# One accumulator, and a last stage on chip, at the end of a mixture-of-experts layer

## The chip, the cores and the metric

The kernel runs on one core of one Trainium2 chip. The number that counts is device time in microseconds (us), as the median of three runs. All times inside the kernel come from one profiled execution and are counted from its first instruction. Engines are named as the profile names them: PE is the matmul engine (PEld its weight loads), DVE the vector engine, ACT the scalar engine, POOL the GpSimd engine, SP the sync engine, which here only issues DMAs.

## The reference, cut to what matters

The block is a token mixer followed by a mixture of experts (MoE) on 512 tokens of 1024 values. Only the end of the MoE is touched by the change:

```python
def _moe(h, ...):                       # 64 experts, each token goes to 8 of them
    ...
    yb = lax.map(expert_block, (xb, block_e)).reshape(n_slots, d)
    routed = jax.ops.segment_sum(yb * slot_w[:, None].astype(yb.dtype), slot_tok, num_segments=t + 1)[:t]
    shared = (jax.nn.silu(xt @ w_sh_gate_l) * (xt @ w_sh_up_l)) @ w_sh_down_l
    return (routed + shared).reshape(b, l, d)
...
    x = x + g2 * _rmsnorm(_moe(h2, *moe_p), norm_ffn_post[i])
```

So every expert's rows are scaled and added to the rows of their tokens; then each token's sum is normalized by its root mean square, multiplied by a vector (`g2p` in the kernel) and added to the token's value from before the MoE (`x1`), which gives the output.

## The kernel before

The MoE works through 65 blocks: one of 128 rows for each of the 64 experts (`e` from 0 to 63), and one extra block (`e == NE`, 64) for the rows that overflow a block. Further overflow blocks, if there are any, run in a loop whose count the chip reads from memory (`For_i(0, cnt)`, L1459). In this data the count is zero: 65 blocks' matmuls stand in the profile.

The loop over `e` is unrolled, and step `e` holds pieces of several blocks: the gate and up projections of block `e` (`proj`), the transposes of block `e+2`'s gathered rows (`make`), the conversion of weights ahead (`convert`), the down projection of block `e-1` (`down`), and the gather of block `e+4`'s rows (`prepare`). Weights come through SP's queue, three blocks ahead; those of the extra block are gathered through POOL's queue. POOL also issues the gathers of rows, and, for each block, an indirect DMA that adds the block's 128 rows into a [512, 1024] accumulator in DRAM (L1272, `compute_op=OP.add`), called the scatter below.

Two accumulators are kept, `accd[0]` and `accd[1]`. The blocks alternate between them, and the last four all go to the second. `accd[0]` begins as the shared expert's output, `accd[1]` as zeros (a memset and four writes, L1152 to L1154). The order of instructions that touch one DRAM tensor is kept by semaphores: a scatter waits until the earlier scatter into the same accumulator has landed.

`accd[0]` is read back (`m0`, L1453) in step 62, together with two of the four tiles of `x1`. After the last scatter comes the loop for further blocks; with a count of zero, every engine jumps over the body and waits until everything issued so far is done. Behind it `accd[1]` is read (L1476), the two sums are added (L1478), squared and summed on ACT (L1481), scaled and raised to the power -1/2 (`rsqrt`: L126 on DVE, L127 on POOL), multiplied (L1484), and added to `x1`: by an adding DMA for two of the four token tiles (L1486), on DVE for the other two (L1488), which are then written (L1489). L1507 is the end of the program, where all engines meet.

`down` splits a block's 1024 columns in two halves in PSUM; DVE scales the first into `y` (L1271), ACT the second (L1269). `pa`, `pi` and `pc` hand out PSUM banks (3, 3 and 2). Instructions of an engine run in the order that the compiler's scheduler gave them, which need not be that of the text; `tc.issue_after(x)` puts an instruction behind `x` on its engine. Matmul operands in `F32R` run in one pass; those in `F32` take more.

Of the kernel before, what the change touches and what calls it, by code (L numbers as in the profile page):

```python
# [19 lines left out]
D = 1024  # L20
# [51 lines left out]
class K:  # L72
# [912 lines left out]
    def phaseO(self):  # L985
# [7 lines left out]
        self.accd = [dp.tile([512, 1024], F32, name=f"acc{i}") for i in range(2)]  # L993
# [79 lines left out]
        def shared_down(t):  # L1073
            y = self.rawp.tile([128, 1024], F32, name="y", tag="raw")
            for c in range(2):
                ps = self.pa()
                for k in range(2):
                    nc.tensor.matmul(ps, sgs[t][:, k * 128:k * 128 + 128], wsh[2][:, k, c * 512:c * 512 + 512], start=k == 0, stop=k == 1)  # L1078
                nc.scalar.copy(y[:, c * 512:c * 512 + 512], ps)
            nc.scalar.dma_start(self.accd[0][t * 128:t * 128 + 128], y)  # L1080
# [77 lines left out]
    def phaseM(self):  # L1158
# [26 lines left out]
        def load(e, n, wix=None):  # L1185
            if e > NE:
                return
            t = raw(e, n)
# [72 lines left out]
        def down(aT, sx, ws, wd, acc):  # L1261
            y = self.rawp.tile([128, 1024], F32, name="y", tag="raw")
            for c in range(2):
# [6 lines left out]
                else:  # L1270
                    ts(y[:, 0:512], ps, ws, None, op0=OP.mult)  # L1271
            nc.gpsimd.indirect_dma_start(self.accd[acc][:, :], bass.IndirectOffsetOnAxis(ap=sx, axis=0), y[:, :], None,  # L1272
                                         bounds_check=511, oob_is_err=False, compute_op=OP.add)

# [140 lines left out]
        def extra_list(wi, px, colx):  # L1415
            ps = self.pi()
            pv = ps[:, 0:6].rearrange("p (e j) -> p e j", e=1)
            onehot_mm(pv[:, 0], lambda c: px[:, c:c + 1], lambda c: colx[:, c, 0])
            sl = [q.tile([128, 1], dt, name=nm, bufs=2) for dt, nm in ((F32, "sl_t"), (I32, "sl_i"), (F32, "sl_w"))]
            slot_of(pv, 1, sl)  # L1420
            return wi, sl[1], sl[2]

        x = lambda e: [XT[e][:, h] for h in range(2)]
        for e in range(NE + 2):
            if e == 3:
                ranks()
# [15 lines left out]
            if e > 0:  # L1442
                down(aT, SL[e - 1], W[e - 1], raw(e - 1, 2), 1 if e - 1 > NE - 4 else (e - 1) % 2)
                load(e + 2, 2)
            make(e + 2, 1)
            prepare(e + 4)
            if e == NE - 2:

                halves = lambda w: [w[:, i * 1024:i * 1024 + 1024] for i in range(2)]
                m0 = halves(raw(e, 0)) + halves(raw(e, 1))  # L1450
                x1 = halves(raw(e + 1, 0)) + halves(raw(e + 1, 1))
                for t in range(4):
                    nc.sync.dma_start(m0[t], self.accd[0][t * 128:t * 128 + 128])  # L1453
                for t in range(2, 4):
                    nc.sync.dma_start(x1[t], self.out[t * 128:t * 128 + 128])


        cnt = nc.values_load(nx[0:1, 0:1], min_val=0, max_val=62)
        with tc.For_i(0, cnt) as _:  # L1459
            wi, ix, ws = extra_list(*extra_cols())  # L1460
            xT, xg = xtile(), gather(ix)
            for c in range(2):
                turn(xT, c, xg)
            for n in range(3):
                load(NE, n, wi)
            w = [conv(raw(NE, n), tt, 1024) for n in range(2)]
# [3 lines left out]
            down(turn_act(act(pgu[:, 0:256], pgu[:, 256:512])), ix, ws, raw(NE, 2), 1)  # L1470


        m = halves(raw(NE, 0)) + halves(raw(NE, 1))
        r = q.tile([128, 4], F32, name="fr")
        for t in range(4):
            (nc.scalar if t % 2 else nc.sync).dma_start(m[t], self.accd[1][t * 128:t * 128 + 128])  # L1476
        for t in range(4):
            tt(m[t], m[t], m0[t], op=OP.add)  # L1478
            self.d("moe", m[t], t)
            junk = q.tile([128, 1024], BF, name="xT", bufs=2)  # L1480
            nc.scalar.activation(junk, m[t], AF.Square, accum_out=r[:, t:t + 1])  # L1481
            self.rsqrt(r[:, t:t + 1], r[:, t:t + 1], 1.0 / D, EPS)
        for t in range(4):
            nc.vector.scalar_tensor_tensor(m[t], m[t], r[:, t:t + 1], g2p, op0=OP.mult, op1=OP.mult)  # L1484
            if t < 2:
                nc.gpsimd.dma_start(self.out[t * 128:t * 128 + 128], m[t], accum_op=OP.add)  # L1486
            else:
                tt(m[t], m[t], x1[t], op=OP.add)  # L1488
                (nc.scalar if t % 2 else nc.sync).dma_start(self.out[t * 128:t * 128 + 128], m[t])  # L1489
# [22 lines left out]
```

## Time and profile before

| | |
|---|---|
| median of 3 runs | 1406.16 us (1405.65 to 1406.91) |
| the profiled execution, whole | 1415.91 us |
| its span, first to last instruction | 1414.1 us |
| busy share of the span: PE, DVE, ACT, POOL | 94%, 64%, 46%, 29% |
| last matmul ends at | 1381.5 us |

The profiled execution is 0.7% longer than the median, and 1.8 us of it lie outside the span. Shares of the whole span hide that nothing runs on PE in the last 32 us.

### The profile page before, as it was taken

The page shows a single profiled execution, that of the slowest core. Times are in us where ns is not written, and L with a number is a line of the kernel's source. Part 1 is how long each engine was busy: PE and PEld are TensorE (multiplying, and loading weights), DVE is VectorE, ACT ScalarE, POOL GpSimd, SP SyncE. Part 2 cuts the span into 40 slices and gives each one's busy share as a digit, 9 for nine tenths or more (in the row PEclk, how much of TensorE's full clock was granted, in tenths as well). Part 3 has the DMA queues.
Part 4 walks back from the last instruction along what each step waited for, and adds up shares of the span by engine and source line. Part 5 has one row for each costly group of instructions (what it writes and reads, how often), then busy time and mean ns, then how long its engine had stood idle before and what let it go on. Part 6 is the DMA issues. An engine that isn't in the chain of part 4 may idle for free.

```text
span 1414.1 us, 20716 instructions
## 1 busy us (share of the span) xinstructions
PE 1324.8 (94%) x7848; PEld 1074.7 (76%) x7848; DVE 906.7 (64%) x1270; ACT 653.4 (46%) x926; POOL 409.6 (29%) x330
## 2 busy tenths in 40 slices
PE   6999988899999999999999999999999999999990
PEld 1678866798787777778888787878788888878770
DVE  5645796457676555547668666666666666666543
ACT  5533432553333222334355555555656565555531
POOL 0315544865321000003222222222222222224312
PEclk9899998999999999999999999999999999999995
DMA  7554411102316577575699999999999999999954
GB/s 275 181 141 117 121 56 35 52 16 74 88 49 179 178 214 223 152 259 195 249 386 349 352 370 345 373 351 364 362 366 361 368 364 361 367 364 338 326 183 127
DMA packets 137817, 340.51 MB, mean 241 GB/s; under 512 B 28218, under 2 KB 83038, under 8 KB 112756
## 3 DMA queue, kind: packets, MB, share of 16 engines
q1 hardware_dynamic: 110952, 289.46, 57.2%
q0 software_dynamic: 19584, 38.99, 10.9%
q10 hardware_dynamic: 7180, 10.72, 2.2%
q8 instruction: 63, 1.03, 0.3%
q14 instruction: 38, 0.31, 0.1%
HBM read 326.59 MB, written 48.31 MB: 265 GB/s over the span
## 4 chain that ended last, share of the span: by engine, by line
PE 43%; DMA 7%; issue 1%; ACT 1%; POOL 1%; DVE 0%; DVEq 0%; SPq 0%; ACTq 0%; POOLq 0%
PE cs L1267 13%; PE acc L111 7%; PE acc L113 7%; PE acc L112 7%; DMA w<-in_w_up_dram 4%; PE ci L1236 3%; DMA w<-in_w_gate_dram 2%; PE ci L1066 2%; PE acc L1078 1%; PE acc L1256 1%; DMA w<-acc 1%; POOL fr L127 0%; DMA acc<-y,slots 0%; DMA acc<-y,sl_i 0%; ACT wh L1171 0%
## 5 line engine op out<-in xcount | busy, mean ns | idle before, releaser
L111 PE MATMUL acc<-wh,xT 128*128 128x256 f32 x1040 | 302.2, 291 | 0.0
L113 PE MATMUL acc<-wh,xT 128*128 128x256 f32 x1040 | 291.0, 280 | 0.0
L112 PE MATMUL acc<-wl,xT 128*128 128x256 f32 x1040 | 290.6, 279 | 0.0
L1173 DVE TENSOR_TENSOR wl<-w,wh 128x2048 fp32r<-128x2048 f32 x88 | 201.5, 2291 | 76.2 <-PE acc L112 75.2
L1267 PE MATMUL cs<-wd,aT 128*128 128x512 f32 x520 | 234.6, 594 | 4.5 <-DMA wd<-in_w_down_dram 3.6
L1272 POOL DMA_INDIRECT acc<-y,slots x64 | 101.9, 1593 | 466.5 <-ACT y L1269 427.8
L1171 ACT CAST wh<-w 128x2048 fp32r<-128x2048 f32 x88 | 167.5, 1904 | 99.5 <-PE acc L113 70.2
L111 PEld LDWEIGHTS acc<-wh,xT 128*128 128x128 f32 x1040 | 196.6, 189 | 0.2 <-issue 0.2
L112 PEld LDWEIGHTS acc<-wl,xT 128*128 128x128 f32 x1040 | 196.1, 189 | 0.2 <-issue 0.2
L113 PEld LDWEIGHTS acc<-wh,xT 128*128 128x128 f32 x1040 | 195.5, 188 | 0.0
L1267 PEld LDWEIGHTS cs<-wd,aT 128*128 128x128 f32 x520 | 93.8, 190 | 99.0 <-issue 95.1
L1239 DVE TENSOR_TENSOR xT<-ci,xT 128x512 fp32r<-128x512 f32 x130 | 89.2, 687 | 96.5 <-ACT xT L1238 96.1
L100 ACT CAST wu<-raw 128x1024 fp32r<-128x1024 f32 (+1 forms) x73 | 75.1, 1036 | 104.6 <-DMA raw<-in_w_in_dram 68.0
L111 PE MATMUL acc<-hTx,wu 128*128 128x512 f32 (+1 forms) x296 | 119.6, 404 | 1.5 <-ACT wu L100 1.5
L113 PE MATMUL acc<-hTx,wu 128*128 128x512 f32 (+1 forms) x296 | 117.7, 398 | 1.5 <-DVE wu L107 1.5
L1173 DVE TENSOR_TENSOR wl<-wgu,wh 128x2048 fp32r<-128x2048 f32 x42 | 96.2, 2291 | 34.6 <-PE acc L112 34.4
L112 PE MATMUL acc<-hLx,wu 128*128 128x512 f32 (+1 forms) x296 | 117.1, 396 | 0.0
L107 DVE TENSOR_TENSOR wu<-raw,wu 128x1024 fp32r<-128x1024 f32 (+1 forms) x61 | 78.7, 1299 | 55.4 <-ACT wu L100 55.4
L1171 ACT CAST wh<-wgu 128x2048 fp32r<-128x2048 f32 x42 | 79.8, 1901 | 53.5 <-PE acc L113 35.5
L1236 PEld LDWEIGHTS ci<-ident,xg 128*128 128x128 f32 x520 | 72.5, 191 | 30.6 <-issue 30.2
L1228 POOL DMA_INDIRECT xg<-h2d,slots x64 | 75.5, 1180 | 35.6 <-issue 18.0
L1236 PE MATMUL ci<-ident,xg 128*128 128x128 f32 x520 | 78.7, 275 | 0.1
(493 smaller groups left out, 2374.3 us busy)
## 6 DMA issues: line engine op xcount, KB each, us to landing
wd<-in_w_down_dram SPq DMA_DIRECT2D x64, 1024.0 KB
w<-in_w_gate_dram SPq DMA_DIRECT2D x43, 1024.0 KB
w<-in_w_up_dram SPq DMA_DIRECT2D x43, 1024.0 KB
raw<-in_w_in_dram SPq DMA_DIRECT2D x56, 512.0 KB
wgu<-in_w_gate_dram SPq DMA_DIRECT2D x21, 1024.0 KB
wgu<-in_w_up_dram SPq DMA_DIRECT2D x21, 1024.0 KB
mraw<-in_w_mod_dram SPq DMA_DIRECT2D x32, 512.0 KB
wm<-in_w_mod_dram SPq DMA_DIRECT2D x16, 512.0 KB
```

Source lines behind the costliest of these rows:

```text
L100: nc.scalar.copy(dst, src)
L107: (self.nc.gpsimd if eng == "pool" else self.nc.vector).tensor_tensor(dst, src, hi.bitcast(F32), op=OP.subtract)
L111: mm(out, ah, bh, start=start, stop=False)
L112: mm(out, ah, bl, start=False, stop=False)
L113: mm(out, al, bh, start=False, stop=stop)
L1171: nc.scalar.copy(h[:, i:i + max(n, 1024)], w[:, i:i + max(n, 1024)])
L1173: eng(l[:, i:i + n], w[:, i:i + n], h[:, i:i + n].bitcast(F32), op=OP.subtract)
L1228: nc.gpsimd.indirect_dma_start(xg[:, :], None, self.h2d[:, :], bass.IndirectOffsetOnAxis(ap=ix, axis=0), bounds_check=511, oob_is_err=False)
L1236: nc.tensor.transpose(ps[:, k * 128:k * 128 + 128], xv[:, :, c * 4 + k], self.ident)
L1239: tt(l, ps, h.bitcast(F32), op=OP.subtract)
L1267: nc.tensor.matmul(ps, aT[:, m], wd[:, s], start=k == 0, stop=k == 1)
L1272: nc.gpsimd.indirect_dma_start(self.accd[acc][:, :], bass.IndirectOffsetOnAxis(ap=sx, axis=0), y[:, :], None, bounds_check=511, oob_is_err ...
```

## The change

There is one accumulator, which begins as the shared expert's output. Blocks 0 to 62 are scattered into it as before. Blocks 63 and 64 are not scattered: `down_parts` keeps their scaled rows on chip, each as a high part in one-pass format and a low part (the rest), `places` makes for each of them four one-hot matrices (slot by token of a token tile), and `finish` multiplies the two and so puts the rows where their tokens are, in PSUM, where both blocks add up. The accumulator is read when the scatter of block 62 has landed, `x1` in step 63. Per token tile DVE then adds PSUM to what was read, and normalization, product and sum follow; DVE's instructions stand in a written order (`then`), with one of four products by `g2p` on POOL. The loop for further blocks comes last and carries a `finish` of its own.

```diff
-        self.accd = [dp.tile([512, 1024], F32, name=f"acc{i}") for i in range(2)]
+        self.accd = dp.tile([512, 1024], F32, name="acc")
...
-        z = self.rawp.tile([128, 1024], F32, name="zero", tag="raw")
-        nc.gpsimd.memset(z, 0.0)
-        for t in range(4):
-            nc.scalar.dma_start(self.accd[1][t * 128:t * 128 + 128], z)
...
+        def down_parts(aT, ws, wd):
+            y = T8("yhl")
+            for c in range(2):
+                ps = self.pc()
+                for k in range(2):
+                    s, m = slice(k * 1024 + c * 512, k * 1024 + c * 512 + 512), slice(k * 128, k * 128 + 128)
+                    nc.tensor.matmul(ps, aT[:, m], wd[:, s], start=k == 0, stop=k == 1)
+                h, l = y[:, c * 512:c * 512 + 512], y[:, 1024 + c * 512:1536 + c * 512]
+                nc.scalar.activation(h, ps, AF.Copy, scale=ws)
+                nc.vector.scalar_tensor_tensor(l, ps, ws, h.bitcast(F32), op0=OP.mult, op1=OP.subtract)
+            return y
+
+        def places(oh, row):
+            at = q.tile([128, 4], F32, name="at", bufs=2)
+            for t in range(4):
+                ts(at[:, t:t + 1], row, -128.0 * t, None, op0=OP.add)
+                ts(oh[:, t], cst("r0"), at[:, t:t + 1], None, op0=OP.is_equal)
+
+        def finish(m, x1, blocks):
...
+            def place(t, j):
+                oh, y = blocks[j]
+                for c in range(2):
+                    if j == 0:
+                        PS[t, c] = self.pc() if t == 3 else self.pi() if c else self.pa()
+                    for i in range(2):
+                        nc.tensor.matmul(PS[t, c], oh[:, t], y[:, i * 1024 + c * 512:i * 1024 + c * 512 + 512],
+                                         start=j == 0 and i == 0, stop=j == len(blocks) - 1 and i == 1)
+
+            for t in (0, 1):
+                place(t, 0)
+            for t in range(4):
+                if t > 1:
+                    place(t, 0)
+                for j in range(1, len(blocks)):
+                    place(t, j)
...
+            def add(t):
+                for c in range(2):
+                    s = slice(c * 512, c * 512 + 512)
+                    then(lambda: tt(m[t][:, s], PS[t, c], m[t][:, s], op=OP.add))
+                self.d("moe", m[t], t)
+                junk = q.tile([128, 1024], BF, name="xT", bufs=2)
+
+                nc.scalar.activation(junk, m[t], AF.Square, scale=D ** -0.5, accum_out=r[:, t:t + 1])
+                nc.scalar.activation(r[:, t:t + 1], r[:, t:t + 1], AF.Identity, bias=self.eps)
+                if t == 1:
+                    nc.gpsimd.tensor_tensor(mg[t], m[t], g2p, op=OP.mult)
+                nc.gpsimd.tensor_tensor(r[:, t:t + 1], r[:, t:t + 1], self.mhalf, op=OP.pow)
+
+            def scaled(t):
+                then(lambda: tt(mg[t], m[t], g2p, op=OP.mult))
+
+            def out(t, s, eng):
+                then(lambda: nc.vector.scalar_tensor_tensor(mg[t][:, s], mg[t][:, s], r[:, t:t + 1], x1[t][:, s], op0=OP.mult, op1=OP.add))
+                eng.dma_start(self.out[t * 128:t * 128 + 128, s], mg[t][:, s])
+
+            whole = slice(0, 1024)
+            add(0)
+            scaled(0)
+            add(1)
+            out(0, whole, nc.sync)
+            add(2)
+            scaled(2)
+            add(3)
+            out(1, whole, nc.scalar)
+            scaled(3)
+            out(2, whole, nc.sync)
+            out(3, slice(0, 512), nc.scalar)
+            out(3, slice(512, 1024), nc.sync)
...
+            if e == NE:
+                OH = T8("oh").rearrange("p (b t n) -> p b t n", b=4, t=4)
+                OH = [OH[:, 0], OH[:, 1]]
+                row = q.tile([128, 1], F32, name="row", bufs=1)
+                nc.vector.tensor_copy(row, slots[:, NE - 1:NE])
+                places(OH[0], row)
+                places(OH[1], self.xrow)
...
-            if e > 0:
-                down(aT, SL[e - 1], W[e - 1], raw(e - 1, 2), 1 if e - 1 > NE - 4 else (e - 1) % 2)
+            if e > NE - 1:
+                Y.append(down_parts(aT, W[e - 1], raw(e - 1, 2)))
+            elif e > 0:
+                down(aT, SL[e - 1], W[e - 1], raw(e - 1, 2))
                 load(e + 2, 2)
...
-            if e == NE - 2:
...
+            if e == NE - 1:
+                x1 = halves(NE - 1)
                 for t in range(4):
-                    nc.sync.dma_start(m0[t], self.accd[0][t * 128:t * 128 + 128])
-                for t in range(2, 4):
                     nc.sync.dma_start(x1[t], self.out[t * 128:t * 128 + 128])
+            if e == NE:
+                m = halves(NE)
+                for t in range(4):
+                    nc.sync.dma_start(m[t], self.accd[t * 128:t * 128 + 128])
+
+        finish(m, x1, list(zip(OH, Y)))
 
 
         cnt = nc.values_load(nx[0:1, 0:1], min_val=0, max_val=62)
         with tc.For_i(0, cnt) as _:
...
+            finish(m, x1, [(oh, down_parts(turn_act(act(pgu[:, 0:256], pgu[:, 256:512])), ws, to[2]))])
```

The old end of the program behind the loop (L1474 to L1489) is removed.

## Rows read from the trace of the kernel before

**Rows 1.** Busy time by stretch: engines' busy us (instructions), PEclk, DMA share, GB/s.

```profile
1200.00:1250.00 50.00, 50.00 (x326) 40.75 (x326) 33.70 (x30) 29.72 (x35) 13.16 (x10) 1.00 1.01 366
1300.00:1350.00 50.00, 46.97 (x297) 37.38 (x297) 30.39 (x27) 25.38 (x29) 16.45 (x10) 1.00 0.87 298
1380.00:1390.00 10.00, 1.46 (x4) 0.38 (x2) 0.53 (x1) 0.69 (x1) 1.56 (x1) 0.68 0.20 27
1390.00:1400.00 10.00, 0.00 (x0) 0.00 (x0) 4.42 (x5) 3.03 (x5) 0.69 (x1) 0.50 0.52 207
1400.00:1414.10 14.10, 0.00 (x0) 0.00 (x0) 7.87 (x10) 1.55 (x4) 5.83 (x6) 0.50 0.62 149
```

**Rows 2.** The chain that ended last, from 1375 us: start, us, what.

```profile
1377.71 4.65 DMA acc<-y,slots
...
1383.19 4.62 DMA acc<-y,sl_i
...
1389.12 8.80 DMA w<-acc
...
1399.32 3.21 POOL fr L127 x3
...
1406.28 1.14 DVE w L1488
```

**Rows 3.** Timeline of POOL, steady loop and its end: start, us, instruction, [idle before <-releaser].

```profile
1108.86 1.59 POOL L1272 DMA_INDIRECT acc<-y,slots  x1 [7.26 <-ACT y L1269]
1110.76 1.04 POOL L1228 DMA_INDIRECT xg<-h2d,slots  x1 [0.30 <-issue]
1119.05 1.59 POOL L1272 DMA_INDIRECT acc<-y,slots  x1 [7.26 <-ACT y L1269]
...
1359.26 1.58 POOL L1272 DMA_INDIRECT acc<-y,slots  x1 [0.31 <-issue]
1369.86 1.56 POOL L1272 DMA_INDIRECT acc<-y,slots  x1 [9.02 <-DMA acc<-y,slots]
```

**Rows 4.** DMA queues, 1111.3 to 1118.4 us, then 1118.4 to 1121.7: packets, MB, share.

```profile
q0 software_dynamic: 253, 0.35, 21.3%
...
q0 software_dynamic: 35, 0.04, 3.7%
```

**Rows 5.** Waits of ACT, 1250 to 1380 us: total us, times, longest.

```profile
ACT wh L1171 <- DMA w<-in_w_up_dram: 19.1, 4, 5.7
ACT wh L1171 <- DMA wgu<-in_w_up_dram: 10.9, 3, 6.2
```

**Rows 6.** What the removed initialization of the second accumulator took.

```profile
L1154 ACTq DMA_DIRECT2D acc<-zero x4: 326/500/1214, 690.2 to 693.5; - x4
L1152 POOL MEMSET zero<- x1: 998/998/998, 680.3 to 680.3; 128x1024 f32 x1
```

**Rows 7.** Timeline from 1370 us: the last block's down projection, and evictions.

```profile
1377.76 3.70 PE L1267 MATMUL cs<-wd,aT 128*128 128x512 f32 x8 [0.82 <-ACT aT L1258]
...
1379.78 0.75 DVE L1271 TENSOR_SCALAR y<-cs,sl_w 128x512 f32<-128x512 f32 x1 [3.99 <-PE cs L1267]
...
1381.49 0.69 ACT L1269 ACTIVATE y<-cs,sl_w 128x512 f32<-128x512 f32 x1 [3.79 <-PE cs L1267]
```

**Rows 8.** Timeline of DVE and ACT behind the loop.

```profile
1393.08 2.36 DVE L1478 TENSOR_TENSOR w<-w,wgu 128x1024 f32<-128x1024 f32 x2 [12.55 <-DMA w<-acc]
1405.00 1.28 DVE L1484 SCALAR_TENSOR_TENSOR w<-w,fr,g2p 128x1024 f32<-128x1024 f32 x1 [0.43 <-POOL fr L127]
1406.20 2.35 DVE L1488 TENSOR_TENSOR w<-w 128x1024 f32<-128x1024 f32 x2
...
1394.34 1.06 ACT L1481 ACTIVATE xT<-w 128x1024 bf16<-128x1024 f32 x1 [12.15 <-DVE w L1478]
```

**Rows 9.** Two prices: DVE with one PSUM input; DVE and POOL side by side.

```profile
L1239 DVE TENSOR_TENSOR xT<-ci,xT x130: 677/691/694, 708.4 to 1358.9; 128x512 fp32r<-128x512 f32 x130
...
637.58 0.69 DVE L1115 TENSOR_TENSOR h<-mix,mrow 128x512 f32<-128x512 f32 x1
637.62 1.80 POOL L1116 TENSOR_TENSOR h<-mix,mrow 128x512 f32<-128x512 f32 x1 [1.40 <-DVE mix L1112]
...
480.79 1.30 POOL L976 TENSOR_TENSOR y<-y 128x512 f32<-128x512 f32 x1 [52.45 <-DVE y L974]
```

**Rows 10.** A matmul of 256 columns on the chain (one pass): start, us from one to the next.

```profile
1373.16 0.12 PE acc L113
```

**Rows 11.** Instructions of the loop's exit and of the program's end: ns min/median/max, first and last start.

```profile
L1459 SPq EVENT_SEMAPHORE  x12: 28/28/28, 1387.8 to 1388.5; - x12
L1459 PEldq COMPARE_BRANCH  x3: 101/185/336, 1378.5 to 1389.3; - x3
...
L1507 SPq DRAIN  x3: 7/7/7, 1413.2 to 1413.6; - x3
```

More of the change, by code (lines that the diff above doesn't have):

```diff
@@ L1079, in shared_down @@
                 nc.scalar.copy(y[:, c * 512:c * 512 + 512], ps)
-            nc.scalar.dma_start(self.accd[0][t * 128:t * 128 + 128], y)
+            nc.scalar.dma_start(self.accd[t * 128:t * 128 + 128], y)
         self.shared = lambda t: (shared_up(t), shared_down(t))
@@ L1183, in phaseM, with load @@
         raw = lambda e, n: DW[e % 3] if n == 2 else GU[(2 * e + n) % 6]
-        def load(e, n, wix=None):
+        def load(e, n, wix=None, to=None):
             if e > NE:
                 return
-            t = raw(e, n)
+            t = raw(e, n) if to is None else to
             if e == NE:
@@ L1259, in turn_act, with down @@
             return aT
-        def down(aT, sx, ws, wd, acc):
+        def down(aT, sx, ws, wd):
             y = self.rawp.tile([128, 1024], F32, name="y", tag="raw")
@@ new lines, in places, with then @@
+        def places(oh, row):
[4 more added lines that the diff above has]
+        def finish(m, x1, blocks):
+            mg = [T[:, i * 1024:i * 1024 + 1024] for T in [self.wt8([128, 2048], F32, "mg", "b") for _ in range(2)] for i in range(2)]
+            r = q.tile([128, 4], F32, name="fr")
+            PS = {}
+            def place(t, j):
[13 more added lines that the diff above has]
+                    place(t, j)
+            last = [None]
+            def then(f):
+                if last[0] is None:
+                    last[0] = f()
+                else:
+                    with tc.issue_after(last[0].ins):
+                        last[0] = f()
+            def add(t):
[27 more added lines that the diff above has]
+            out(3, slice(512, 1024), nc.sync)
@@ L1420, in extra_list @@
             slot_of(pv, 1, sl)
+            self.xrow = sl[0]
             return wi, sl[1], sl[2]
         x = lambda e: [XT[e][:, h] for h in range(2)]
+        halves = lambda e: [raw(e, n)[:, i * 1024:i * 1024 + 1024] for n in range(2) for i in range(2)]
+        Y = []
         for e in range(NE + 2):
+            if e == NE:
[5 more added lines that the diff above has]
+                places(OH[1], self.xrow)
             if e == 3:
@@ L1446, in phaseM @@
             prepare(e + 4)
-            if e == NE - 2:
-                halves = lambda w: [w[:, i * 1024:i * 1024 + 1024] for i in range(2)]
-                m0 = halves(raw(e, 0)) + halves(raw(e, 1))
-                x1 = halves(raw(e + 1, 0)) + halves(raw(e + 1, 1))
+            if e == NE - 1:
+                x1 = halves(NE - 1)
                 for t in range(4):
-                    nc.sync.dma_start(m0[t], self.accd[0][t * 128:t * 128 + 128])
-                for t in range(2, 4):
                     nc.sync.dma_start(x1[t], self.out[t * 128:t * 128 + 128])
+            if e == NE:
[3 more added lines that the diff above has]
+        finish(m, x1, list(zip(OH, Y)))
         cnt = nc.values_load(nx[0:1, 0:1], min_val=0, max_val=62)
@@ L1460, in phaseM @@
             wi, ix, ws = extra_list(*extra_cols())
+            oh = T8("oh").rearrange("p (b t n) -> p b t n", b=4, t=4)[:, 0]
+            places(oh, self.xrow)
             xT, xg = xtile(), gather(ix)
@@ L1463, in phaseM @@
                 turn(xT, c, xg)
+            to = [raw(NE - 2, 0), raw(NE - 2, 1), raw(NE, 2)]
             for n in range(3):
-                load(NE, n, wi)
-            w = [conv(raw(NE, n), tt, 1024) for n in range(2)]
+                load(NE, n, wi, to[n])
+            w = [conv(to[n], tt, 1024) for n in range(2)]
             pgu = self.pa()
@@ L1469, in phaseM @@
                 proj(pgu[:, n * 256:n * 256 + 256], [xT[:, h] for h in range(2)], w[n])
[L1470 to L1489, printed above, removed]
+            finish(m, x1, [(oh, down_parts(turn_act(act(pgu[:, 0:256], pgu[:, 256:512])), ws, to[2]))])
         self.pes.close()
```

2 lines of the change are left out of this document (1 added, 1 removed).

## The prediction

> **What bounds the kernel now.** I read the stretches first, then the chain of waits at the end, then the timelines of single engines around both.
>
> The stretches split the MoE in three [rows 1]. Up to about 1260 us PE is busy all the time (50.00 of 50 us) with the DMA engines at a share of 1.01: PE sets the pace, one block each 10.2 us (scatters at 1108.86 and 1119.05, [rows 3]), and the weights fall slowly behind. From 1300 to 1350 us PE has holes (46.97 of 50), because ACT waits for weights [rows 5]: DMA sets the pace. From 1381.5 us, when the last down projection ends [rows 7], PE does nothing, and what is left is a tail of 1414.1 - 1381.5 = 32.6 us.
>
> The chain shows what the tail is made of [rows 2]: the scatter of block 63 (4.65 us), that of block 64 behind it (4.62), the loop's exit, the read of the accumulator (8.80), then DVE and POOL in turns until DVE's last instruction ends at 1408.55 (two from 1406.20 in 2.35 us, [rows 8]), and 5.55 us of writing and ending. So two round trips to DRAM, one after the other, stand between the last matmul and the first sum at 1393.08; DVE is busy for 12.8 of the last 34 us. A change in the tail is worth its full time; one in the loop only where it touches PE before 1260 us or DMA after that.
>
> **The change part by part.**
>
> *Zeros left out.* One memset of 1.0 us on POOL and four writes, issued between 690.2 and 693.5 us [rows 6]. They are ahead of the steady stage, PE is not waiting for them, and the accumulator's first scatter comes 37 us later. Worth nothing; the upper bound of a gain is their issue time on ACT, about 2 us.
>
> *One accumulator: an added wait.* Each scatter now waits for the landing of the scatter just before it, where so far it waited for the last but one. Behind it on POOL stand the gather of rows and, at the end, the extra block's weights; PE's transposes wait for those gathers. The steady loop shows the margin: the scatter of 1108.86 had its packets done by about 1118.4 (253 packets of that queue up to there, 35 in the 3.3 us after it, which are mostly the gather's; [rows 4]), so some 9.5 us after its issue, and the next is issued at 1119.05, when ACT has its rows ready. That is 0.65 us of margin. The one pair that is serialized under load today is that of blocks 61 and 62: issue to issue 1369.86 - 1359.26 = 10.6 us, ended by the landing [rows 3]. Without load the pair 63 and 64 took 1383.19 - 1377.71 = 5.5 us. So a step of the chain of scatters costs 5.5 to 10.6 us against a pace of 10.2. I take about 10.2 on average: scatter and gather share one queue that has hardly a pause, so a scatter that is issued 0.5 us later finds less of the gather still in front of it. POOL then runs late by a few us, more in some steps and less in others. What covers that: a gather issued in step e is used in step e+2, 20 us later, and lands about 11 us after its issue (1110.76 to 1121.7), so POOL may be about 9 us late before PE notices, and a little PE time lost before 1260 us comes back, since DMA sets the pace after that. Cost taken: 0; bounds below, in the second rival.
>
> *Reads moved.* The 2 MB of `m0` leave step 62; four tiles of `x1` take their place on SP a moment earlier, with 1 MB less in all. The last scatter (block 62) has landed by 1377 at the latest as things stand: its rows are issued at 1369.86, and an unhurried scatter takes 4.65 [rows 2, 3]. Four reads of the accumulator follow on SP. Their price is the 8.80 us of today's, so 1386 for the last tile, and less for the first; the sums of the four tiles need them at 1384, 1386, 1390 and 1392 (below). Hidden, unless POOL is more than about 4 us late.
>
> *Blocks 63 and 64 on chip.* Block 63's parts are made while PE still works: ACT has pauses of over 3 us there, DVE too [rows 7]. `places` puts 17 small DVE instructions into step 64, where DVE is mostly idle. For block 64: PE ends at 1381.46, ACT makes the last high part (0.69 us, to 1382.2), DVE the low part (0.69 to 0.75 us, the row with one PSUM input and the row that scales; to 1383.0) [rows 7, 9]. PE meanwhile places block 63 for two token tiles: 8 matmuls of 512 columns. No row has this matmul in this stage; a 256-column one follows the next in 0.117 us [rows 10], twice that is 0.23, and four-fold work of `F32` in L1267 gives 3.70/8 = 0.46 as the upper bound. With 0.23: 1.9 us, to 1383.3. Four more matmuls finish the first tile at 1384.2, its first half at 1383.8. From there PE needs 8 x 0.23 = 1.9 us a tile and DVE about 3.6, so DVE sets the pace.
>
> *DVE's list.* Eight sums of 512 columns with one PSUM input at 0.69 [rows 9]: 5.5. Three products of 1024 columns at 1.22 (two in 2.36 to 2.44): 3.7. Three last steps at 1.28 and two halves at 0.66: 5.2 [rows 8]. Together 14.4; instructions back to back overlap by 0.08 us (two of 1.22 take 2.36), over 16 of them 1.3, so 13.1. Waits on top: the first `r` needs ACT's square (1.06 + 0.2 + 0.2) and POOL's power (0.55 to 1.5), and is ready about 0.7 us after DVE wants it; POOL's product of 1024 columns is twice 1.30 to 1.80, 2.6 to 3.6 us [rows 9], and `out(1)` needs it and a power behind it at 1393, which just about fits. Beside a DVE product POOL took 1.80 us for what takes 1.30 alone, and DVE kept its 0.69. The Trainium skill (SBUF — State Buffer, "SBUF: two separate sides") says that a GpSimd instruction and a DVE instruction with two SBUF inputs lock each other out of a shared port, whoever comes first. The row agrees for POOL as the later one; by the rule DVE too could stand for up to a whole POOL product. With no lock on DVE the waits are 0.7 us, with a full one 0.7 + 3.6 = 4.3; I take 1.5, nearer to the row. DVE ends at 1384.1 + 13.1 + 1.5 = 1398.7, against 1408.55.
>
> *The end.* From DVE's last instruction to the end it takes 5.55 us today. The last write is now half as large, 0 to 1.3 us less, taken 0.4. The loop now stands behind the writes. Its body is skipped, but each engine waits there for everything that is under way: today SP's checks run from 1387.8, the landing of the scatter, to 1388.5, and PE's queue leaves at 1389.3 plus 0.3 [rows 11]. So 0.9 to 1.9 us more between the last landing and the end, taken 1.5. End: 1398.7 + 5.55 - 0.4 + 1.5 = 1405.35.
>
> **Sum.** 1414.1 - 1405.35 = 8.75 us off the profiled span (1415.91 with what lies around it). The profiled execution is 0.7% longer than the median, and I take the same difference off the median: 1406.16 - 8.75 = 1397.4 us. With all small terms at their low ends (waits 0, exit 0.9, write 1.3 less): 1394.4. With them at the high ends, and PE's placements put by the scheduler ahead of block 64's down projection (2 us later): 1384.1 + 2 + 13.1 + 4.3 + 5.55 + 1.9 = 1410.95, 3.2 us off: 1403.0.
>
> **Rivals.**
>
> 1. *The tail is freed of DRAM, but DVE and POOL take turns.* `out(0)` stands in DVE's fixed order ahead of `add(2)`, so every late `r` or POOL product stops all that follows. For it: today's chain has POOL's powers in it for 3.21 us [rows 2]. Against it: three other DVE instructions lie between most pairs. Two such stops of 2 to 3 us: about 1401.
>
> 2. *The single accumulator makes the chain of scatters the pace; slower than before.* If each step cost the 10.6 us of the loaded pair, POOL would lose 0.4 us a block. The 9 us of gather slack would be gone after some 23 blocks, and the other 40 would go at POOL's pace: 16 us lost on PE, of which DMA's lateness after 1260 takes back about 8; and POOL, still late, would read the accumulator 5 to 9 us late in the tail. That is 13 to 17 us against the 8.75: 1410 to 1414, slower. It decides from a mean step of about 10.5 us. For it: the loaded pair, and a margin of only 0.65 us. Against it: POOL never waited for a landing in the steady stage, and the queue is shared with the gather. A milder form (mean step 10.3, POOL some 6 us late at the end) costs 2 to 5 us: 1400 to 1402.
>
> 3. *The end saves more:* reads early, sums at full pace and writes overlapped: 1393 to 1394.5.
>
> **How the numbers follow.** The forecast as worked out, 1397.4, gets 0.68; the first rival 0.13; the second's mild form 0.06 and its full form 0.07; the third 0.06. 0.2% of the median is 2.8 us, about what a measurement of this kernel can tell from no change, so "same" is 1403.3 to 1409.0. Faster: 0.68 + 0.13 + 0.06 + 0.06, less a little of their upper ends: 0.91. Same: 0.05. Slower: 0.04. The range leaves out the full form of the second rival, and the third: 1394.4 to 1402.5.
>
> **What would show it.** Right, if: the last matmul ends at about 1388 to 1389 and PE is busy up to it; DVE's first sum starts near 1384 with the accumulator already read; DVE's last instruction ends 9 to 10 us earlier than before; the span ends some 6.5 us after it; in the steady loop POOL's scatters do wait for landings now, but PE stays without holes up to 1260. Wrong, if: the steady pace is above 10.2 us a block; PE's transposes wait for gathers; DVE waits in the tail for reads of the accumulator, for POOL's product, or for `r`, for more than 2 us together; or the engines spend more than 3 us between the last landing and the end.

## The result, and the profile after

The changed kernel is slower. In the timed comparison it took 1422.88 us (median of 6 runs) against 1406.54 us (6 runs): ratio 1.0108, 95% interval 1.0069 to 1.0147, so +15 us where 8.75 less was forecast. The profiled execution took 1422.77 us, with a span of 1420.6.

The tail came out as forecast. These are the rows after the change that answer to [rows 7, 8]: PE's last down projection, then DVE and POOL.

```profile
1393.21 3.62 PE L1278 MATMUL cs<-wd,aT 128*128 128x512 f32 x8
...
1398.27 0.68 DVE L1325 TENSOR_TENSOR w<-acc,w 128x512 f32<-128x512 f32 x1
...
1402.18 3.32 POOL L1332 TENSOR_TENSOR mg<-w,g2p 128x1024 f32<-128x1024 f32 x1 [0.38 <-DVE w L1325]
...
1404.53 2.06 DVE L1336 TENSOR_TENSOR mg<-w,g2p 128x1024 f32<-128x1024 f32 x1
...
1408.90 1.21 DVE L1336 TENSOR_TENSOR mg<-w,g2p 128x1024 f32<-128x1024 f32 x1
...
1410.04 2.60 DVE L1339 SCALAR_TENSOR_TENSOR mg<-mg,fr,w 128x1024 f32<-128x1024 f32 x3
```

From the end of the last down projection (1396.84) to the end of the span (1420.64) it is 23.8 us; before it was 32.7. That is 8.9 us less. But the last down projection itself starts at 1393.21 instead of 1377.76, although the first expert's projection started earlier (708.1 us against 712.9). The loss lies in the loop between them: 688.7 us from the first projection to the end of the last down projection, against 668.6. 20.2 more and 8.9 less are 11.3 us, inside the interval of the timed ratio (+9.7 to +20.7); the two profiled spans differ by less, 6.5, because that execution of the kernel before reached its first projection 4.8 us later, 3.5 of it within the first 40 us, far ahead of anything that was changed.

There POOL's waits have changed their name. Group of the scatters on the page (busy us and mean ns of one, then idle time before it and what ended most of it):

```profile
L1268 POOL DMA_INDIRECT acc<-y,slots x63 | 117.1, 1859 | 437.4 <-DMA acc<-y,slots 107.1
```

Waits after the change, 720 to 1380 us (total us, times, longest):

```profile
POOL acc L1268 <- DMA acc<-y,slots: 107.1, 15, 9.0
...
POOL acc L1268 <- ACT y L1265: 58.0, 9, 7.7
...
PE ci L1232 <- DMA xg<-h2d,slots: 14.3, 6, 5.1
```

Before, the scatter waited for ACT's rows [rows 3]; now it waits for the landing of the scatter ahead, and PE's transposes wait for gathers, which they never did. The steps on POOL's timeline are longer than PE's pace, in three answers from the start, middle and end of the loop:

```profile
839.89 1.59 POOL L1268 DMA_INDIRECT acc<-y,slots  x1 [7.75 <-ACT xT L1234]
...
872.16 1.59 POOL L1268 DMA_INDIRECT acc<-y,slots  x1 [6.73 <-DMA acc<-y,slots]
...
882.77 1.59 POOL L1268 DMA_INDIRECT acc<-y,slots  x1 [7.08 <-DMA acc<-y,slots]
...
1177.27 1.59 POOL L1268 DMA_INDIRECT acc<-y,slots  x1 [7.02 <-DMA acc<-y,slots]
...
1188.19 3.27 POOL L1268 DMA_INDIRECT acc<-y,slots  x1 [7.68 <-DMA acc<-y,slots]
...
1371.30 1.57 POOL L1268 DMA_INDIRECT acc<-y,slots  x1 [8.82 <-DVE wl L1169]
```

882.77 - 872.16 is 10.61 us and 1188.19 - 1177.27 is 10.92. Over the 49 steps from 839.89 to 1371.30 the mean is 10.85 us; PE needs some 10.2. (Where the row names another engine than the landing, that engine had long been done: from block 11 on all scatters but two are issued 0.80 to 0.87 us after the landing of the one before.) PE doesn't lose at once: it waits for no gather before 1080 us, and from block 11 (834.88) to block 34 (1071.09) its down projections follow each other at 10.27 us, although the scatters are chained all that time. The landing times of that line, from issue, 860 to 1250 us:

```profile
L1268 POOL DMA_INDIRECT acc<-y,slots x36: 1587/1588/3635, 861.3 to 1244.0; - x36
...
DMA to landing us min/median/max: 7.2/10.1/14.5
```

And what it does to PE, by stretch (columns as in [rows 1]):

```profile
1060.00:1160.00 100.00, 94.87 (x601) 76.65 (x600) 61.97 (x55) 54.06 (x64) 31.62 (x19) 0.98 0.97 339
1160.00:1260.00 100.00, 94.69 (x593) 75.69 (x593) 62.01 (x54) 54.16 (x63) 33.03 (x18) 0.98 0.97 336
1200.00:1250.00 50.00, 44.69 (x277) 35.30 (x276) 28.05 (x25) 24.49 (x30) 18.00 (x10) 0.97 0.94 318
1300.00:1350.00 50.00, 46.15 (x283) 36.61 (x282) 29.73 (x26) 26.10 (x32) 23.79 (x11) 0.97 0.91 300
```

From 1200 to 1250 PE was busy for 50.00 us [rows 1] and is now for 44.69, with the DMA engines at 0.94 instead of 1.01: neither of the two old bounds is the bound any more. (PEclk is 0.97 to 0.98 of the upper level, 2.4 GHz, in stretches in which PE has holes, and 1.00 in [rows 1].)

### The profile page after: what moved, and what is told of

Its sections match the earlier page's. It is cut to its first block, busy times and chain, and to the rows that moved or that the text cites. A ratio compares the mean times of both kernels' runs of the same rounds, so it can differ in the third digit from the quotient of the medians.

```text
span 1420.6 us, 20809 instructions
## 1 busy us (share of the span) xinstructions
PE 1338.7 (94%) x7880; PEld 1085.7 (76%) x7880; DVE 912.4 (64%) x1291; ACT 656.5 (46%) x932; POOL 452.9 (32%) x326
## 5 line engine op out<-in xcount | busy, mean ns | idle before, releaser
L1169 DVE TENSOR_TENSOR wl<-w,wh 128x2048 fp32r<-128x2048 f32 x88 | 201.7, 2293 | 88.0 <-PE acc L112 87.9
L1268 POOL DMA_INDIRECT acc<-y,slots x63 | 117.1, 1859 | 437.4 <-DMA acc<-y,slots 107.1
L1263 PE MATMUL cs<-wd,aT 128*128 128x512 f32 x504 | 230.9, 602 | 0.0
L1169 DVE TENSOR_TENSOR wl<-wgu,wh 128x2048 fp32r<-128x2048 f32 x42 | 96.3, 2293 | 41.3 <-PE acc L112 40.1
L1224 POOL DMA_INDIRECT xg<-h2d,slots x64 | 106.1, 1658 | 36.5 <-DVE slots L1214 17.5
L1232 PE MATMUL ci<-ident,xg 128*128 128x128 f32 x520 | 80.3, 279 | 14.3 <-DMA xg<-h2d,slots 14.3
```

The costliest lines, as they stand in the source:

```text
L1169: eng(l[:, i:i + n], w[:, i:i + n], h[:, i:i + n].bitcast(F32), op=OP.subtract)
L1224: nc.gpsimd.indirect_dma_start(xg[:, :], None, self.h2d[:, :], bass.IndirectOffsetOnAxis(ap=ix, axis=0), bounds_check=511, oob_is_err=False)
L1232: nc.tensor.transpose(ps[:, k * 128:k * 128 + 128], xv[:, :, c * 4 + k], self.ident)
L1263: nc.tensor.matmul(ps, aT[:, m], wd[:, s], start=k == 0, stop=k == 1)
L1268: nc.gpsimd.indirect_dma_start(self.accd[:, :], bass.IndirectOffsetOnAxis(ap=sx, axis=0), y[:, :], None, bounds_check=511, oob_is_err=Fals ...
```

## The experiments

**Theory:** the single accumulator makes a chain of scatters (landing, 0.80 us, next issue) that is slower than PE; POOL falls behind by some 0.6 us a block, and PE loses time once the gathers, which stand behind the scatters on POOL, have used up their slack. **Rivals:** the new end costs the time (its program, its reads); or each serialized scatter costs PE its share at once, whatever the slack. (The second is already hard to hold against the trace above, where PE keeps its pace for 23 chained steps.)

All results in one table. "Loop" is from the first expert's projection to the end of the last down projection, "tail" from there to the end of the span, both from the profiled execution; the ratio is that of the timed runs to the kernel before on the same chip, and is not exactly the quotient of the medians.

| kernel | median us (runs) | ratio, 95% interval | loop us | tail us |
|---|---|---|---|---|
| before | 1406.54 (6) | | 668.6 | 32.7 |
| changed | 1422.88 (6) | 1.0108 (1.0069 to 1.0147) | 688.7 | 23.8 |
| e1 two accumulators, new end | 1409.41 (12) | 1.0010 (0.9994 to 1.0026) | 675.8 | 23.8 |
| e2 one accumulator, old end | 1424.69 (6) | 1.0121 (1.0091 to 1.0152) | 685.3 | 29.3 |
| e3 meant: gathers a step earlier; in fact the changed kernel's order | 1422.80 (6) | 1.0090 (1.0067 to 1.0113) | 694.0 | 23.8 |
| e4 as e1, sum left out | 1404.12 (7) | 0.9958 (0.9941 to 0.9974) | 670.9 | 23.8 |
| e5 as e4, tiles moved 32 bytes | 1400.38 (6) | 0.9934 (0.9913 to 0.9956) | 670.3 | 23.8 |
| e6 before, tiles moved 96 bytes | 1413.83 (12) | 1.0028 (1.0014 to 1.0042) | 671.6 | 32.8 |
| e7 as e5, sum on PE | 1406.39 (12) | 0.9985 (0.9969 to 1.0000) | 670.4 | 26.9 |
| e8 as e7, one block in eight apart | 1408.84 (12) | 1.0004 (0.9984 to 1.0023) | 675.2 | 27.7 |
| e9 two accumulators, added by DMA, tiles in place | 1400.25 (6) | 0.9951 (0.9935 to 0.9967) | 668.7 | 24.5 |
| e10 changed, tiles in place | 1422.32 (5) | 1.0111 (1.0096 to 1.0127) | 690.6 | 23.8 |
| e11 as e9, no loop behind | 1398.24 (5) | 0.9934 (0.9921 to 0.9947) | 668.5 | 19.7 |

The kernel before took 1408.54 us (18 runs) beside e1 to e4, 1408.77 (29) beside e5 to e8, and 1408.17 (11) beside e9 to e11. The changed kernel and e3 have the same instructions in the same order, and their loops differ by 5.3 us: where PE waits for gathers, one profiled loop is good to some 5 us only. Where it doesn't, loops agree closely (668.5 to 668.7 in before, e9 and e11).

**e1: the accumulators undone.** The changed kernel with two accumulators (blocks alternate; zeros, `m0` and its read in step 62 are back), and four sums on DVE ahead of `finish`.

```diff
-                down(aT, SL[e - 1], W[e - 1], raw(e - 1, 2))
+                down(aT, SL[e - 1], W[e - 1], raw(e - 1, 2), 1 if e - 1 > NE - 4 else (e - 1) % 2)
...
+        for t in range(4):
+            tt(m[t], m[t], m0[t], op=OP.add)
         finish(m, x1, list(zip(OH, Y)))
```

> The changed kernel with the two accumulators of before put back for blocks 0 to 62; the second one is read at the end, the first one two steps earlier, and DVE adds them (4 x 1.22 us). Theory (each scatter waits for the landing of the one before, a step of that chain takes 10.85 us against PE's pace of 10.2, POOL falls behind and PE's transposes wait for gathers): no waits of PE for gathers left, POOL waits for ACT's rows again, and the tail keeps its gain of 8.8 us less up to 4.9 for the sums: 3 to 9 us faster than before, near 1401. Rival (the loop lost its time through the rest of the change: moved reads, 17 more DVE instructions, slower matmuls): still slower than before by some 10 us or more.

The loop is 13 us shorter than the changed kernel's, and the loss through the gathers is gone, but the 3 to 9 us of gain aren't there: the time can't be told from that of the kernel before. POOL waits for ACT's rows again (429.2 us, 59 times) and PE never for a gather. What ate the gain is in the timelines of e1, first DVE and then PE:

```profile
1377.02 1.23 DVE L1559 TENSOR_TENSOR w<-w,wgu 128x1024 f32<-128x1024 f32 x1 [4.85 <-DMA w<-acc]
1378.16 0.74 DVE L1285 SCALAR_TENSOR_TENSOR yhl<-cs,xg,yhl 128x512 fp32r<-128x512 f32 x1
```

```profile
1378.96 1.22 PE L1306 MATMUL acc<-yhl,oh 128*128 128x512 f32 x2 [3.78 <-DVE yhl L1285]
1379.98 0.63 PE L1306 MATMUL ci<-yhl,oh 128*128 128x512 f32 x1
1380.41 4.59 PE L1282 MATMUL cs<-wd,aT 128*128 128x512 f32 x8
```

The first sum waits 4.85 us for the read of the accumulator. Behind it on DVE stands the low part of block 63, PE's placement waits 3.78 us for that, and block 64's down projection stands behind the placement.

**e2: the accumulator alone.** The kernel before with one accumulator, and nothing of the new end. The zeros, the second read and the four sums go with the second accumulator.

```diff
-        self.accd = [dp.tile([512, 1024], F32, name=f"acc{i}") for i in range(2)]
+        self.accd = dp.tile([512, 1024], F32, name="acc")
```

> The kernel before with one accumulator and nothing else: no zeros, no second read, no sum of the two; its old end behind the loop stays. Theory: the loop loses what the changed kernel's lost, 15 to 20 us in the profile, and the old end saves the four sums only in part: 10 to 20 us slower than before, and POOL waits for landings as in the changed kernel. Rival: within 3 us of before.

+17 us, from this one part of the change: the loop is 16.7 us longer, though the old end without its sums is 3.4 shorter. The waits of e2, 720 to 1380 us, are those of the changed kernel:

```profile
POOL acc L1268 <- DMA acc<-y,slots: 80.8, 12, 9.2
...
PE ci L1232 <- DMA xg<-h2d,slots: 14.4, 5, 4.9
```

**e3: meant as more slack.** The changed kernel with the call that issues a gather moved up by one step in the text.

```diff
+        prepare(4)
...
-            prepare(e + 4)
+            prepare(e + 5)
```

> The changed kernel with each gather issued one block earlier (five blocks ahead instead of four), still behind a scatter that waits. Theory: the chain of scatters keeps its step of about 10.85 us, but PE's transposes have 10 us more to spare, so most of the 14 us that PE waited for gathers goes: 5 to 12 us faster than the changed kernel, unless POOL falls so far behind that the three buffers for scaled rows run out and DVE or ACT wait there. Rival (gathers are not what holds PE): no difference to the changed kernel.

The time is the changed kernel's, but that speaks neither for the theory nor for its rival, because the edit didn't move the gathers. Instructions stand in the scheduler's order, and on every engine that order is the changed kernel's, instruction for instruction. Block 12's gather on POOL and PE's first transpose of its rows, in the changed kernel and then in e3:

```profile
790.04 1.04 POOL L1224 DMA_INDIRECT xg<-h2d,slots  x1 [0.30 <-issue]
813.88 0.62 PE L1232 MATMUL ci<-ident,xg 128*128 128x128 f32 x4
```

```profile
786.48 1.04 POOL L1224 DMA_INDIRECT xg<-h2d,slots  x1 [0.30 <-issue]
810.33 0.62 PE L1232 MATMUL ci<-ident,xg 128*128 128x128 f32 x4
```

It is 23.8 us from issue to use in both. So e3 is a second measurement of the changed kernel (PE waits for gathers for 16.1 us here, 14.3 there), and what a step more of slack would do is not shown.

**e4: the tail's worth.** As e1 without the four sums (the output lacks the first accumulator's rows).

```diff
-        for t in range(4):
-            tt(m[t], m[t], m0[t], op=OP.add)
         finish(m, x1, list(zip(OH, Y)))
```

> As the first of these kernels, but the sum of the two accumulators is left out: the output lacks the shared expert and the blocks in the first accumulator. It prices the tail as the prediction had it, with a loop that is not held up. Theory: 1397 to 1399, that is 8 to 9 us faster than before, and 2 to 5 us faster than the first kernel. Rival: slower than before, like the changed kernel.

0.42% faster than before (5.9 us; 4.4 by the medians), not the 8 to 9 us expected, and 5 us of e1 were the sums. Still, the tail is 8.9 us shorter; the loop is 2.3 us longer than before although POOL waits for nothing new. Its matmuls of 256 columns follow each other at 119 ns instead of 117 (medians over the loop), in the changed kernel, e1, e3 and e4, and not in e2, which has the old end.

**e5 and e6: the place of the tiles.** The new end's small tiles (`at`, `row`) lie in the pool of `xT`, `xg`, `wd` and `aT`, and move these down by 96 bytes. e5 is e4 with 32 bytes more; e6 is the kernel before, with the same instructions in the same order, and its tiles where the changed kernel has them.

```diff
-                row = q.tile([128, 1], F32, name="row", bufs=1)
+                row = q.tile([128, 16], F32, name="row", bufs=1)[:, 0:1]
...
-        r = q.tile([128, 4], F32, name="fr")
+        r = q.tile([128, 40], F32, name="fr", bufs=1)[:, 0:4]
```

> As e4_two_acc_no_sum (two accumulators, new end, the first accumulator's rows left out of the output), with the tile `row` widened from 1 to 16 columns. That moves xT, xg, wd and aT, which lie in the same pool, by 32 bytes, from a multiple of 32 bytes to one of 256; nothing else changes. If the projections' matmuls go at 119 ns instead of 117 because of where the tiles lie, they go at 117 here and the time falls by some 4 us from e4's 1404.1, to about 1400. If the cause is something else in the program (more instructions, the loop's longer body), it stays at 119 ns and 1404.

> The kernel before with one tile (`fr`) made wider, so that the same pool's tiles lie 96 bytes lower, exactly where the changed kernel has them; the instructions are the same ones in the same order. By the place of the tiles: 119 ns a matmul, a pace of 10.27 us a block instead of 10.20, and some 4 us slower than before, 1410 to 1411. By any other cause: the time of before.

e6 is 0.28% slower, 3.9 us, from the addresses alone. Starts of two successive down projections in PE's timeline, of e6, then of e5, then of e9 below:

```profile
1103.67 3.60 PE L1267 MATMUL cs<-wd,aT 128*128 128x512 f32 x8
1113.94 3.60 PE L1267 MATMUL cs<-wd,aT 128*128 128x512 f32 x8
```

```profile
1108.85 3.60 PE L1267 MATMUL cs<-wd,aT 128*128 128x512 f32 x8
1119.10 3.60 PE L1267 MATMUL cs<-wd,aT 128*128 128x512 f32 x8
```

```profile
1106.63 3.60 PE L1267 MATMUL cs<-wd,aT 128*128 128x512 f32 x8
1116.84 3.60 PE L1267 MATMUL cs<-wd,aT 128*128 128x512 f32 x8
```

10.27 us a block where `xT` starts 32 bytes above a multiple of 256 (e6, as in the changed kernel), 10.25 at a multiple of 256 (e5), 10.21 at 128 bytes above one (e9, as before). e5 moved the pace by only a third of what I expected; its timed gain over e4 (0.24%, the intervals overlap) is more than the 0.6 us that its loop shows, and may hold a difference between chips.

**e7 and e8: the sum elsewhere, and the chain cut.** e7 is e5 with the first accumulator added on PE, by a product with the identity (8 matmuls of 512 columns). e8 is e7 with only every eighth block in the second accumulator, so that six steps of eight still wait for the landing before.

```diff
+            def other(t):
+                for c in range(2):
+                    nc.tensor.matmul(PS[t, c], self.ident, m0[t][:, c * 512:c * 512 + 512], start=False, stop=True)
...
-                down(aT, SL[e - 1], W[e - 1], raw(e - 1, 2), 1 if e - 1 > NE - 4 else (e - 1) % 2)
+                down(aT, SL[e - 1], W[e - 1], raw(e - 1, 2), (e - 1) % 8 // 7)
```

> The whole computation: two accumulators and the new end, the tiles moved as in e5, and the first accumulator added on TensorE by a product with the identity into the same sums (8 matmuls of 512 columns, F32), in place of four sums on VectorE. In e1 the first of these sums waited for a read of the accumulator and held up the low part of block 63 and with it block 64's down projection for 4 us; here nothing of VectorE waits for a read before the parts are made. TensorE has to do 8 x 0.46 = 3.7 us more in the end, where VectorE sets the pace. Expected: e5 plus 0 to 2 us, 1400 to 1402, so faster than before by some 5 us. If the sums themselves were the price, it would be near e1 less the 4 us of the tiles' place, 1405.

> As e7, but the second accumulator takes one block in eight (7, 15, ... 55) instead of every second; six steps in eight are then serialized as with a single accumulator. If the single accumulator costs time because the chain of scatters (10.85 us a step) slowly uses up the slack of the gathers, the two free steps in each eight let GpSimd catch up the 6 x 0.65 = 4 us before the slack is gone, and the time is that of e7. If each serialized step cost TensorE its share at once (16 us over 60 steps), six eighths of that, 10 to 12 us, would be lost: 1411 to 1413.

e7 took 6 us more than e5, not 0 to 2. I had the price of an `F32` matmul wrong: the row of 3.70 us in [rows 7] counts 8 records, but they are 4 matmuls, so one is 0.9 us, not 0.46. PE's part of the tail grew by 6.9 us (13.3 against 6.4), and DVE waits for it: the tail is 3.1 us longer.

e8 lost 2.4 us to e7 in the timed runs (with intervals that overlap; 4.8 in the profiled loops), not the 10 to 12 us of the rival by which each wait costs its share. POOL's timeline around a free step of e8:

```profile
869.07 1.59 POOL L1272 DMA_INDIRECT acc<-y,slots  x1 [6.29 <-DVE xT L1239]
...
877.91 1.59 POOL L1272 DMA_INDIRECT acc<-y,slots  x1 [4.87 <-ACT y L1269]
...
888.15 1.59 POOL L1272 DMA_INDIRECT acc<-y,slots  x1 [7.32 <-ACT y L1269]
```

Up to 869.07 POOL had fallen 1.4 us behind; the next scatter goes to the other accumulator 8.84 us later, when ACT's rows are ready, and POOL is level again. Waits of e8, 720 to 1380 us:

```profile
POOL acc L1272 <- ACT y L1269: 160.4, 23, 8.3
POOL acc L1272 <- DMA acc<-y,slots: 77.3, 9, 14.4
...
PE ci L1236 <- DMA xg<-h2d,slots: 4.1, 2, 3.5
```

Landings still hold up POOL for 77.3 us, yet PE waits for a gather only twice, and both times near 1300 us, where the slack (landing of a gather to its use by PE), about 11 us around 1050, had fallen to 0.04. So a wait costs PE nothing while slack is left, and the used-up slack does. That it did fall shows that one free step in eight doesn't quite do: the serialized steps took 11 to 12 us and more there, and two scatters in flight at once took 14 to 16.5 us each to land.

**e9, e10 and e11: what is left.** e9 has two accumulators, `row` widened to 48 columns (tiles in their old place), and the second accumulator added by the transfers that read it, onto the tiles of the first. e10 is the changed kernel with `row` widened in the same way. e11 is e9 without the loop over further blocks, which runs zero times here.

```diff
-                m = halves(NE)
+                m = m0
                 for t in range(4):
-                    nc.sync.dma_start(m[t], self.accd[1][t * 128:t * 128 + 128])
+                    nc.gpsimd.dma_start(m[t], self.accd[1][t * 128:t * 128 + 128], accum_op=OP.add)
```

> The whole computation: two accumulators and the new end; the second accumulator is not read into tiles of its own and summed, but added by the transfer itself (issued by GpSimd, four of them) onto the tiles that hold the first; and `row` is widened to 48 columns, so that xT and its neighbours start 128 bytes above a multiple of 256, as before the change. If the end is worth what it took in e4 and e5 (23.8 us behind the last down projection instead of 32.6) and only the place of the tiles and the sum stood against it, this is some 7 to 9 us faster than before: 1399 to 1401, and the projections' matmuls go at 117 ns. If the adding transfers land late (they follow the scatter of block 62 and are issued one by one), VectorE's first sum waits for them: 1402 to 1405.

> The changed kernel with its single accumulator, and xT and its neighbours moved to where the kernel before has them relative to 256 bytes. The matmuls should go at 117 ns. If the chain of scatters sets the pace of the later blocks, faster matmuls only make TensorE wait longer for the gathers, and the time stays within 2 us of the changed kernel's 1422.9. If instead the two losses add up, it falls by some 4 us, to 1419.

> As e9_added_by_dma, without the loop over further blocks, which runs zero times with these inputs (the kernel would be wrong for inputs that need it). The price of passing the loop's entry and exit behind the last write: the span should end about 5.5 us after VectorE's last instruction as in the kernel before, instead of 8.0, so 1.5 to 2.5 us faster than e9. If the 8.0 us are the writes' landing, nothing changes.

e9 beats both kernels: 0.49% faster than the one before, 1400.25 us. Its loop has the old length, and the sum costs DVE nothing (e9, POOL's timeline, then DVE's):

```profile
1367.80 3.71 POOL L1556 DMA_DIRECT2D wgu<-acc  x4 [5.29 <-DMA acc<-y,slots]
```

```profile
1374.58 0.75 DVE L1285 SCALAR_TENSOR_TENSOR yhl<-cs,sl_w,yhl 128x512 fp32r<-128x512 f32 x1 [0.97 <-ACT yhl L1284]
1375.25 0.68 DVE L1329 TENSOR_TENSOR wgu<-acc,wgu 128x512 f32<-128x512 f32 x1
...
1387.06 2.60 DVE L1343 SCALAR_TENSOR_TENSOR mg<-mg,fr,w 128x1024 f32<-128x1024 f32 x3
```

e10 has 117 ns a matmul again and gains nothing that can be seen (ratio 1.0111, against 1.0108 and, in e3, 1.0090 for the changed kernel's order): where the chain is the pace, faster matmuls only wait longer. In e11 the span ends 3.9 us behind DVE's last instruction (1386.99 to 1390.84), in e9 8.7 us (1389.66 to 1398.36). So passing the loop behind the last writes took 4.9 us in the traces. That is more likely too much than too little: the profiled execution of e11 was the fastest of its runs (1392.61 us), and the timed ratios differ by 0.17%, 2.4 us, with intervals that overlap.

## Why the prediction was wrong

**The step that failed** is *One accumulator: an added wait*: "I take about 10.2 on average ... Cost taken: 0". Measured: 10.85 us a step. Two things were wrong in it. First, I took the end of the packets (9.5 us after issue, [rows 4]) for the moment at which the next scatter can start. It starts 0.8 us after the landing, and the rows showed that: 1377.71 + 4.65 is 1382.36, and the next scatter starts at 1383.19 [rows 2]. With it there was no margin of 0.65 us, but one of -0.1. Second, a scatter that is issued later didn't land sooner: from issue to landing the mean over blocks 20 to 50 was 9.83 us before and 10.01 after. 9.83 + 0.80 is 10.63, above the 10.5 from which I had said that the second rival decides, and next to the 10.6 of the loaded pair, which I had put down as a bound.

**What lateness adds.** A scatter that waits for a landing is issued at a moment that PE's pace doesn't set, and may meet DVE's subtraction `wl` (L1169, two inputs in SBUF). Two such meetings in the changed kernel, DVE first:

```profile
1067.63 2.29 DVE L1169 TENSOR_TENSOR wl<-w,wh 128x2048 fp32r<-128x2048 f32 x1 [1.29 <-PE acc L112]
...
1187.71 2.29 DVE L1169 TENSOR_TENSOR wl<-wgu,wh 128x2048 fp32r<-128x2048 f32 x1 [1.29 <-PE acc L112]
```

```profile
1067.75 3.63 POOL L1268 DMA_INDIRECT acc<-y,slots  x1 [7.20 <-DMA acc<-y,slots]
```

The first scatter ends at 1071.38, 1.46 us after the subtraction (1069.92); so does the second, at 1188.19 + 3.27 = 1191.46 against 1190.00. Of the 49 scatters of blocks 11 to 59, 14 were issued during such a subtraction, and each of them ended 1.46 to 1.49 us after it; the other 35 took 1.59 to 1.61 us on POOL. The 11 that took over 2 us landed after 11.35 us on average, the other 38 after 9.63, so these meetings make some 0.4 us of the mean step. In the kernel before none of the scatters met the subtraction, nor in any other kernel here with two alternating accumulators; every kernel with a single one has such meetings. Whether PE would lose its pace without them is open, for no run takes them away: with 9.63 + 0.80 = 10.43 us a step against its 10.27, 49 steps would use up 8 us of 13 us of slack (an estimate from these numbers), with the 9.83 + 0.80 from above all of it.

**The cover** ("about 9 us late before PE notices") was real, and e8 lived on it, but a cover against a loss in every step is only a delay: in the changed kernel the gathers' slack fell from 13 us (block 11) to 0.5 (block 37). "A little PE time lost before 1260 us comes back" was wrong too: nothing came back, since the chain, not DMA, was still the pace at the end.

**The second rival's full form** (1410 to 1414, chance 0.07) was the mechanism. (All of that form is slower than "same", so the 0.04 given to slower contradicted its 0.07.) Of the 16 us that it takes off PE, 8 were to come back by DMA; PE was behind by 18.3 us at block 50 and by 20.3 at block 64, so on balance none came back. Some 2 us of it, up to block 30, are the slower matmuls (e6), not the chain. Its late read of the accumulator cost the tail nothing: block 62's scatter was late, but so was all the rest.

**The tail** was right: 23.8 us against a forecast of 23.9 (1405.35 - 1381.46). In parts: the first sum 1.4 us behind the last down projection (forecast 2.6; the scheduler put four placements of block 63 ahead of it); DVE's list 14.4 us (forecast 13.1 + 1.5); from DVE's end to the end of the span 8.0 us (forecast 6.65, the loop's exit being dearer than the 1.5 taken, by e11). Reads of the accumulator held nothing up. That the whole fits to 0.1 us is in part luck: two parts 1.2 and 0.2 us short of the forecast and one 1.35 over it cancel. The bound of 0.46 us for a placing matmul was misread as in e7; the 0.23 that was taken held (starts at 1398.06, 1398.29 and 1398.52).

**DVE beside POOL.** DVE's product at 1404.53 took 2.06 us where the same one at 1408.90 took 1.21; POOL's product of the same shape was under way until 1405.50. In [rows 9] DVE came first and kept its time, here POOL did and DVE lost 0.85. The Trainium skill (SBUF — State Buffer, "SBUF: two separate sides") says that whichever starts first has the shared port for its whole instruction; this row agrees, for DVE too. The 1.5 us taken for waits held it.

**Not in the prediction at all** was the place of the tiles: 3.9 us in e6, hidden in the changed kernel behind the chain (e10), but due as soon as the chain is gone (e4). **Zeros left out** was not tried alone; the first projection starts at 704.1 to 708.1 us in the four traces without them and at 702.7 to 712.9 in the nine with them, so no gain shows.

## What to carry to other kernels

A wait that comes round every step is priced as a rate, not as a margin: take the mean from issue to landing under load, add the time from landing to the next issue, and compare it with the pace; if it is longer and the loop long enough, slack only sets when the loss starts. Parts of a change are best bought apart: the end on chip made the tail 9 us shorter, the single accumulator that came with it cost 17, and two accumulators whose sum is made by the reading transfer keep the first without the second. An edit that adds a few bytes to a pool moves its other tiles, so compare the spacing of an untouched inner loop before and after. And an edit that moves a line of the text need not move the instruction: look for it in the trace before reading the time (e3).

## What the hardware showed unexpectedly

- The same matmuls in the same order ran at 10.20 to 10.21, 10.25 or 10.27 us a block, as the pool with `xT` started 128, 0 or 32 bytes above a multiple of 256. From the first to the last start of a projection's 24 matmuls it is 2.774, 2.801 and 2.810 us on average (1000 to 1250 us; in e5, at 0 bytes, a block's two projections, which read the same `xT`, take 2.780 and 2.818 by turns). In these matmuls only `xT` was moved; which accesses meet is open, and so is whether another tile of the pool plays a part.
- A serialized scatter follows the landing of the one ahead at 0.80 us, nearly without spread (0.80 to 0.87), loaded or not; late in the loop of e8 two scatters in flight at once landed after 14 to 16.5 us each, where one alone took 10.
- Passing a loop that runs zero times, behind writes under way, took 4.9 us in the traces of e9 and e11, and 2.4 by their timed runs.
- POOL's instruction that issues a scatter takes 1.59 us; when it starts during DVE's subtraction of two SBUF tiles (2.29 us), it ends 1.46 us after that one, in all 14 cases from block 11 to 59 of the changed kernel.
